# Operand parts made at each head's end and passed through DRAM, states in x tiles, embedding copies first

## The chip, the cores and the metric

The kernel runs on one core of a Trainium2 chip. The metric is the device time of one execution in microseconds (us). The core has TensorE (PE, matmuls, with its weight loads shown apart as PEld), VectorE (DVE), ScalarE (ACT), GpSimd (POOL) and SyncE (SP), each with an instruction queue of its own that is worked off in order. A DMA is issued from one of these queues; a DMA instruction that has to wait for something holds up everything behind it in the same queue.

## The reference, cut to what matters

One step of a two-layer decoder on 512 prompt tokens and 8 x 8 sample tokens (576 columns in all). Per layer:

```python
h = rmsnorm(x, pre_g) @ w_in                 # pool inputs and gates, q, k, v, head gates
u = (causal window mean(h_pool) - h_pool) @ w_pool[g] * pool_scale * silu(gate)   # 4 pool groups
q, k = rope(q), rope(k) * DK ** -0.5         # 4 retention heads of width 256
o = masked(q k^T) v + (q S) * q_decay        # S: (8, 4, 256, 256) states for the samples
S_new = exp(C * log_g) * S + (k * k_decay)^T v
o = head_rmsnorm(o) * silu(gate)             # what a head puts out
m = rmsnorm(concat(u, o) @ w_out, post_g)
x = x + m
ple = rmsnorm(p @ w_ple, ple_g)              # per-layer embedding, 256 -> 2048
x = x + ple * sigmoid(x @ w_ple_gate + b)
```

The outputs are y, the new states of all heads and the last pool rows.

## The kernel before

Everything is held with features on the 128 partitions and the 576 tokens along the free axis: a tile is 128x576, and the width of 2048 is 16 tiles. Every weight matmul is made in three passes in fp32r: a value is split into a high part (ACT casts it, line 91) and a low part (DVE subtracts, line 92), and high by high, high by low and low by high are added up in PSUM, in column halves of 288 (HN). `gemm` (line 137) does this plainly; `unit` (lines 117 to 119) works on blocks of two tiles and on sums of blocks (`block_sums`, lines 190 to 193), so that fewer products are needed; `plain_unit` is line 233. Weights come as raw loads of 1 MB into two buffers and are split into `wh` and `wl`.

A layer runs in stages; the times are those of layer 0 in the profiled execution:

- `in_first` (0 to 290 us): the first half of the input projection; its results go to DRAM.
- `in_phase`, heads (290 to 590 us): four calls of `head(h)`. Each finishes its part of the projection, turns q and k, makes scores and outputs, and calls `retention_state` for the sample tokens. That works in two rounds (`bg`) of four states each. A round loads four states of 256 KB into tiles of `s0_ring` (four slots, m24 to m27), multiplies them with q (line 385), makes the k-v products (line 401), adds them onto the states in place (line 402) and stores the states (line 403). So the second round's loads into the same four slots wait for the first round's stores to have read them. At its end a head normalises, multiplies its two output tiles o[0], o[1] by their gates (line 681), stores them in `m_dram` (line 682), makes two tiles of block sums in `x` buffers and stores these too (line 686).
- `in_phase`, pool (590 to 735 us): four calls of `pool_group`. After each, `operands` (line 749) loads one head's two output tiles and two sums into `x` buffers and splits them into seven slots (`own_slots`) for the output projection.
- `out_phase`: the output projection by `unit` (735 to 871 us), the embedding (871 to 909 us), first half of the gate (909 to 1003 us, `gate_step`), second half (1003 to 1105 us, `gated`). Layer 1 follows (1105 to 2194 us).

In the embedding each of 16 tiles is a `gemm` of 12 matmuls. From its two PSUM halves ACT squares (line 342) and then copies into a `part` buffer (line 801), and SP stores that (line 802). PE sums the squares over the partitions (line 304). In `gated`, the stored embedding tile is loaded into an `x` buffer, DVE scales it (828), adds the accumulators (834), ACT makes the sigmoid (836), DVE multiplies and adds (837, 838), and SP stores the result.

Buffers by name: x 4, tmp 4, part 4, d 4, u 6, raw 2, wh 5, wl 5; `rot_ring` is m16 to m23; PSUM has acc 4, pb 2, po 2. The order of the instructions on each engine is set before the run by a scheduler with a cost model of its own: code moved in the source, another buffer or another queue can move any of them. Nearly all DMAs are issued on SP's queue, one of them on ACT's and none on POOL's.

Of the kernel before, what the change touches and what calls it, by code (L numbers as in the profile page):

```python
# [14 lines left out]
P = 128  # L15
# [23 lines left out]
def decoder_kernel(ctx: ExitStack, tc: tile.TileContext, a, decay8):  # L39
# [6 lines left out]
    def buf(tag, shape=(P, NT), dt=F32):  # L46
        return sb.tile(list(shape), dt, tag=tag, name=tag, bufs=BUFS.get(tag, 1))
# [32 lines left out]
    def dram(name, n=KT):  # L80
        return [tc.dram_tile([P, NT], F32, name=f"{name}{i}") for i in range(n)]
# [4 lines left out]
    sums_dram = [dram(f"sums{l}", 8) for l in range(L)]  # L86
# [127 lines left out]
    def operands(xs, pairs=range(4), ops=None, tag="u", slots=own_slots, sums=None):  # L214
        ops = operand_set() if ops is None else ops
        for j in pairs:
            blocks(xs, [j], ops, slots)
            sums_of_blocks(ops, [j], tag, sums=sums)
        return ops
# [155 lines left out]
    def retention_state(l, h, s0_ring, qrep, kst, vst, po_s):  # L375
        for bg in range(2):
            s0s, loads = [], []
            for r in range(4):
                s0 = s0_ring.tile((P, 2, DK))
                loads.append(nc.sync.dma_start(out=s0, in_=a["state_ret"][l, 4 * bg + r, h].rearrange("(t p) e -> p t e", p=P)))  # L380
                s0s.append(s0)
# [115 lines left out]
    def in_phase(l, raws, r2, rB, cos, sin):  # L497
# [90 lines left out]
        def head(h):  # L588
# [91 lines left out]
            for i, g in enumerate(silu_gates(20 + h)):  # L680
                nc.vector.tensor_tensor(out=o[i], in0=o[i], in1=g, op=ALU.mult)
                nc.sync.dma_start(out=m_dram[l][8 + 2 * h + i], in_=o[i])
            sums = [buf("x") for _ in range(2)]
            block_sums(nc.vector, *o, *sums)
            for i, t in enumerate(sums):
                nc.sync.dma_start(out=sums_dram[l][2 * h + i], in_=t)
# [54 lines left out]
        for j, g in enumerate(groups):  # L741
            pool_group(g)
            operands(loader(m_dram[l][8:]), [j], out_ops, sums=loader(sums_dram[l]))
        return out_ops

    def loader(tiles):
        def xs(k):
            t = buf("x")
            nc.sync.dma_start(out=t, in_=tiles[k])
            return t  # L750
        return xs

    def out_phase(l, raws, ops_out):
# [38 lines left out]
        for c8 in range(2):  # L792
            raw = load_weights(a["w_ple"][l, :, c8 * 8:(c8 + 1) * 8].rearrange("p c k n -> p (c k) n"))
            w = split_weights(raw, 0, 16)
            for c in range(8):
# [3 lines left out]
                square(sq, acc)  # L799
                for i in range(2):  # L800
                    nc.scalar.copy(half(t, i), acc[i])
                nc.sync.dma_start(out=ple_dram[l][ct], in_=t)
# [22 lines left out]
        def gated(ct, t, acc, by_half):  # L825
            pl = buf("x")
            nc.sync.dma_start(out=pl, in_=ple_dram[l][ct])
            nc.vector.scalar_tensor_tensor(
# [55 lines left out]
        next_ops = operand_set() if l < L - 1 else None  # L884
        for p in range(8):
# [116 lines left out]
```

## Time and profile before

| what | us |
|---|---|
| three executions, median (lowest to highest) | 2201.31 (2197.42 to 2420.12) |
| the profiled execution | 2196.17 |
| its span in the trace | 2194.4 |
| PE busy | 2169.6 |
| DVE busy | 1721.7 |
| ACT busy | 1061.0 |
| POOL busy | 89.7 |

The span is the time from the first to the last instruction of the profiled execution; the remaining 1.8 us lie around it. Busy is the time in which an engine worked on an instruction; the span less PE's busy time is the time in which no matmul ran. The granted TensorE clock was 1.00 of full speed in every stage.

### The profile page before, as it was taken

Reading aid. Unit: us, or ns where it says so; the run is one execution under the profiler, and the core shown is the slowest. Engines: PE = TensorE matmul, PEld = TensorE weight load, DVE = VectorE, ACT = ScalarE, POOL = GpSimd, SP = SyncE. Lnnn points to the kernel's source line nnn. Section 1 sums busy time; section 2 is a strip of 40 time slices with the busy share of each in tenths; the row PEclk is TensorE's granted clock in tenths of the full one; section 3 lists DMA queues with packets and bytes.
Section 4 is the critical chain, followed back from the end, with each engine's and each line's share of the span. In section 5 each row is a group of like instructions: output and inputs, shape, how many; then the busy total and the mean of one; then the engine's idle time right before and its main releaser. Section 6 shows DMA issues by size and latency. Waiting matters only on the chain.

```text
span 2194.4 us, 42681 instructions
## 1 busy us (share of the span) xinstructions
PE 2169.6 (99%) x16716; PEld 2138.4 (97%) x16716; DVE 1721.7 (78%) x3186; ACT 1061.0 (48%) x2097; POOL 89.7 (4%) x66
## 2 busy tenths in 40 slices
PE   9999999999999999999999999999999999999998
PEld 9999999999999999999999999999999999999998
DVE  8788765767599998888877787666675898988865
ACT  5465533444344555755454554433443445556532
POOL 2000000000001110000110000000000001101000
PEclk9999999999999999999999999999999999999999
DMA  7455455555574433656644544555464743336564
GB/s 233 144 195 167 156 170 158 168 171 172 169 241 150 133 123 119 215 172 217 205 159 151 168 159 151 159 173 169 149 202 148 250 154 122 110 117 228 178 202 146
DMA packets 143337, 371.42 MB, mean 169 GB/s; under 512 B 15008, under 2 KB 53408, under 8 KB 122272
## 3 DMA queue, kind: packets, MB, share of 16 engines
q1 hardware_dynamic: 142992, 368.69, 50.9%
q8 instruction: 131, 2.15, 0.4%
q14 instruction: 70, 0.57, 0.1%
q10 hardware_dynamic: 144, 0.02, 0.0%
HBM read 277.89 MB, written 90.76 MB: 168 GB/s over the span
## 4 chain that ended last, share of the span: by engine, by line
PE 86%; DMA 6%; DVE 4%; issue 1%; ACT 1%; SPq 0%; POOL 0%; DVEq 0%; ACTq 0%; POOLq 0%
PE acc L137 29%; PE acc L117 13%; PE acc L118 13%; PE acc L119 13%; PE acc L233 4%; PE pb L118 3%; PE pb L117 3%; PE pb L119 3%; DMA x<-ple 2%; DMA out_new_ret_s<-m 2%; PE po L137 1%; PE po L385 1%; DVE wl L92 1%; DMA m<-in_state_ret 1%; DVE x L837 1%
## 5 line engine op out<-in xcount | busy, mean ns | idle before, releaser
L137 PE MATMUL acc<-m,wh 128*128 128x288 f32 x3584 | 649.7, 297 | 0.0
L91 ACT CAST wh<-raw 128x512 fp32r<-128x512 f32 x567 | 351.0, 620 | 534.7 <-PE acc L137 274.5
L118 PE MATMUL acc<-m,wh 128*128 128x288 f32 x1944 | 572.6, 295 | 0.0
L117 PE MATMUL acc<-m,wh 128*128 128x288 f32 x1944 | 570.9, 295 | 0.5 <-ACT m L256 0.5
L119 PE MATMUL acc<-m,wl 128*128 128x288 f32 x1944 | 566.5, 295 | 0.0
L137 PEld LDWEIGHTS acc<-m,wh 128*128 128x128 f32 x3584 | 531.8, 188 | 7.1 <-issue 6.2
L92 DVE TENSOR_TENSOR wl<-raw,wh 128x512 fp32r<-128x512 f32 x567 | 400.9, 708 | 122.7 <-ACT wh L91 118.7
L137 PE MATMUL acc<-m,wl 128*128 128x288 f32 x1792 | 391.4, 295 | 0.0
L117 PEld LDWEIGHTS acc<-m,wh 128*128 128x128 f32 x1944 | 364.5, 188 | 1.5 <-ACT m L256 1.0
L118 PEld LDWEIGHTS acc<-m,wh 128*128 128x128 f32 x1944 | 365.0, 188 | 0.0
L119 PEld LDWEIGHTS acc<-m,wl 128*128 128x128 f32 x1944 | 362.5, 188 | 0.2 <-DVE wl L92 0.2
L91 ACT CAST wh<-S 128x512 fp32r<-128x512 f32 x356 | 220.9, 620 | 239.0 <-PE acc L118 146.1
L137 PEld LDWEIGHTS acc<-m,wl 128*128 128x128 f32 x1792 | 290.0, 188 | 1.4 <-issue 1.4
L92 DVE TENSOR_TENSOR wl<-S,wh 128x512 fp32r<-128x512 f32 x356 | 253.1, 713 | 22.6 <-ACT wh L91 21.5
L246 POOL TENSOR_TENSOR S<-raw 128x512 f32<-128x512 f32 x45 | 70.7, 1572 | 1912.0 <-DMA raw<-in_w_out 752.7
L512 DVE TENSOR_TENSOR part<-acc,part 128x288 f32<-128x288 f32 x192 | 79.1, 451 | 73.7 <-PE acc L137 73.1
L246 DVE TENSOR_TENSOR S<-raw 128x512 f32<-128x512 f32 x133 | 93.4, 702 | 19.0 <-DMA raw<-in_w_in 17.5
L118 PE MATMUL pb<-m,wh 128*128 128x288 f32 x324 | 95.5, 295 | 0.0
L117 PE MATMUL pb<-m,wh 128*128 128x288 f32 x324 | 95.1, 294 | 0.0
L119 PE MATMUL pb<-m,wl 128*128 128x288 f32 x324 | 95.0, 293 | 0.0
L256 ACT COPY d<-acc 128x288 f32<-128x288 f32 x228 | 86.2, 395 | 0.0
L261 DVE TENSOR_TENSOR d<-d,acc 128x288 f32<-128x288 f32 x114 | 51.3, 450 | 36.0 <-PE acc L119 35.6
(269 smaller groups left out, 3286.1 us busy)
## 6 DMA issues: line engine op xcount, KB each, us to landing
raw<-in_w_in SPq DMA_DIRECT2D x95, 1024.0 KB, 5.4
raw<-in_w_out SPq DMA_DIRECT2D x32, 1024.0 KB, 4.9
raw<-in_w_gate SPq DMA_DIRECT2D x32, 1024.0 KB, 5.5
proj<-d SPq DMA_DIRECT2D x96, 288.0 KB, 2.1
part<-proj SPq DMA_DIRECT2D x96, 288.0 KB, 3.2
m<-in_state_ret SPq DMA_DIRECT2D x64, 256.0 KB, 3.0
out_new_ret_s<-m SPq DMA_DIRECT2D x64, 256.0 KB, 5.1
x<-m SPq DMA_DIRECT2D x48, 288.0 KB, 3.4
```

The source lines that it names most:

```text
L91: nc.scalar.copy(hi, src)
L92: return nc.vector.tensor_tensor(out=lo, in0=src, in1=hi.bitcast(F32), op=ALU.subtract)
L117: nc.tensor.matmul(out, wh, xh, start=start, stop=False, **kw)
L118: nc.tensor.matmul(out, wh, xl, start=False, stop=False, **kw)
L119: nc.tensor.matmul(out, wl, xh, start=False, stop=stop, **kw)
L137: nc.tensor.matmul(acc[h], u, v[:, h * HN:(h + 1) * HN], start=(i == 0 and passno == 0), stop=(i == n - 1 and passno == 2),)
L233: nc.tensor.matmul(acc[h], w[:, j], xs[h][passno == 1], start=(i == 0 and j == 0 and passno == 0), stop=(i == 1 and j == 3 and passno == 2),)
L246: eng.tensor_tensor(out=s, in0=x, in1=y, op=op)
L256: ops["tail_act"] = nc.scalar.copy(dst, src)
L261: return nc.vector.tensor_tensor(out=dst, in0=dst, in1=src, op=ALU.add)
L385: mm = nc.tensor.matmul(po_s[32 * r:32 * r + 32, bg], qrep[:, dt, b * 32:b * 32 + 32], s0s[r][:, dt], start=(dt == 0), stop=(dt == 1),)
L512: nc.vector.tensor_tensor(out=half(t, h), in0=acc[h], in1=half(t, h), op=ALU.add)
```

## The change

- At a head's end the two sums go to `tmp` buffers. The first half of o[0], o[1] and the two sums are split there into high and low parts, in `x` buffers: seven tiles of 128x576 (the first holds both parts of a half). They are stored in DRAM (`operand_dram`), by DMAs on POOL's queue. o[0] and o[1] themselves and the sums are no longer stored.
- After each pool group `load_operands` loads the seven tiles of one head into the seven slots, again on POOL's queue, and nothing is split there.
- The second round of four states goes into `x` buffers and not into `s0_ring`.
- In the embedding ACT copies first, POOL's queue stores the copy, and the square is made from the copy in SBUF, as one operation of 576 columns.
- In the second half of the gate the embedding tiles are loaded by code that stands two tiles ahead.

```diff
--- before.py
+++ after.py
@@ -83,7 +83,7 @@
     x_dram, m_dram = dram("x"), [dram(f"m{l}") for l in range(L)]
     ple_dram = [dram(f"ple{l}") for l in range(L)]
     gate_dram = [dram(f"gate{l}") for l in range(L)]
-    sums_dram = [dram(f"sums{l}", 8) for l in range(L)]
+    operand_dram = [[tc.dram_tile([P, NT], F32R, name=f"operand{l}_{i}") for i in range(28)] for l in range(L)]
     proj_dram = [dram(f"proj{l}", 48) for l in range(L)]
 
     def split(hi, lo, src, scale=None):
@@ -211,11 +211,11 @@
                 ops[n2].append((hi[:, HN:], lo[:, HN:]))
         return ops
 
-    def operands(xs, pairs=range(4), ops=None, tag="u", slots=own_slots, sums=None):
+    def operands(xs, pairs=range(4), ops=None, tag="u", slots=own_slots):
         ops = operand_set() if ops is None else ops
         for j in pairs:
             blocks(xs, [j], ops, slots)
-            sums_of_blocks(ops, [j], tag, sums=sums)
+            sums_of_blocks(ops, [j], tag)
         return ops
 
     def plain_unit(raw, ops, d0, d1):
@@ -376,7 +376,7 @@
         for bg in range(2):
             s0s, loads = [], []
             for r in range(4):
-                s0 = s0_ring.tile((P, 2, DK))
+                s0 = buf("x", (P, 2, DK)) if bg else s0_ring.tile((P, 2, DK))
                 loads.append(nc.sync.dma_start(out=s0, in_=a["state_ret"][l, 4 * bg + r, h].rearrange("(t p) e -> p t e", p=P)))
                 s0s.append(s0)
             for dt in range(2):
@@ -679,11 +679,29 @@
 
             for i, g in enumerate(silu_gates(20 + h)):
                 nc.vector.tensor_tensor(out=o[i], in0=o[i], in1=g, op=ALU.mult)
-                nc.sync.dma_start(out=m_dram[l][8 + 2 * h + i], in_=o[i])
-            sums = [buf("x") for _ in range(2)]
+            sums = [tmp() for _ in range(2)]
             block_sums(nc.vector, *o, *sums)
-            for i, t in enumerate(sums):
-                nc.sync.dma_start(out=sums_dram[l][2 * h + i], in_=t)
+            both = buf("x", (P, 2, HN), F32R)
+            split(both[:, 0], both[:, 1], o[0][:, :HN])
+            nc.gpsimd.dma_start(out=operand_dram[l][7 * h], in_=both.rearrange("p a n -> p (a n)"))
+            for i, src in enumerate([o[1]] + sums):
+                parts = [buf("x", (P, NT), F32R) for _ in range(2)]
+                split(*parts, src)
+                for k, part in enumerate(parts):
+                    nc.gpsimd.dma_start(out=operand_dram[l][7 * h + 1 + 2 * i + k], in_=part)
+
+        def load_operands(j, ops):
+            new = own_slots(j)
+            tiles = []
+            for i in range(7):
+                t = new[i]((P, NT))
+                nc.gpsimd.dma_start(out=t, in_=operand_dram[l][7 * j + i])
+                tiles.append(t)
+            ops["b11"].append((tiles[0][:, :HN], tiles[0][:, HN:]))
+            for i, names in enumerate((("b21", "b22"), ("t1", "t2"), ("t3", "t4"))):
+                hi, lo = tiles[1 + 2 * i:3 + 2 * i]
+                for h, name in enumerate(names):
+                    ops[name].append((half(hi, h), half(lo, h)))
 
         def pool_group(g):
             w = WINDOWS[g]
@@ -740,7 +758,7 @@
         out_ops = operand_set()
         for j, g in enumerate(groups):
             pool_group(g)
-            operands(loader(m_dram[l][8:]), [j], out_ops, sums=loader(sums_dram[l]))
+            load_operands(j, out_ops)
         return out_ops
 
     def loader(tiles):
@@ -796,10 +814,10 @@
                 ct = c8 * 8 + c
                 acc = gemm(w[2 * c:2 * c + 2], pp)
                 t, sq = buf("part"), buf(("tmp", "tmp", "tmp", "tmp", "g", "g", "u", "u")[ct % 8])
-                square(sq, acc)
                 for i in range(2):
                     nc.scalar.copy(half(t, i), acc[i])
-                nc.sync.dma_start(out=ple_dram[l][ct], in_=t)
+                nc.gpsimd.dma_start(out=ple_dram[l][ct], in_=t)
+                last_square[0] = nc.scalar.activation(sq, t, AF.Square)
                 squares.append(sq)
                 if len(squares) == 4:
                     together(sums, squares, ct == 3, ct == KT - 1)
@@ -822,9 +840,15 @@
             stats["ss"] = buf("long")
         rP = buf("long")
 
-        def gated(ct, t, acc, by_half):
+        def load_embedding(ct):
             pl = buf("x")
             nc.sync.dma_start(out=pl, in_=ple_dram[l][ct])
+            return pl
+
+        def gated(ct, t, acc, by_half):
+            if ct + 2 < KT:
+                pls.append(load_embedding(ct + 2))
+            pl = pls[ct]
             nc.vector.scalar_tensor_tensor(
                 out=pl, in0=pl, scalar=vec["ple_g"][:, l, ct:ct + 1], in1=rP, op0=ALU.mult, op1=ALU.mult
             )
@@ -882,6 +906,7 @@
             return mo[k]
 
         next_ops = operand_set() if l < L - 1 else None
+        pls = [load_embedding(ct) for ct in range(2)]
         for p in range(8):
             raw = raws.pop(("gate2", p))
             for c in range(2):
```

On the whole SP has 96 DMAs fewer and POOL 144 more. Where the order moves:

PE in head 0 of layer 0 before: the first round of states (m_4423 to m_4429) in its last rows; then the projection goes on, and the second round stands 64 rows further down.

```order
L385 MATMUL po<-m_4427,u 32x256
L385 MATMUL po<-m_4429,u 32x256
L401 MATMUL pb<-u 128x256 x2
L137 MATMUL acc<-m_1850,wh 128x288 x2
L137 MATMUL acc<-m_1851,wh 128x288 x2
L137 MATMUL acc<-m_1850,wl 128x288 x2
```

PE at the same place after:

```order
L385 MATMUL po<-m_4467,u 32x256
L385 MATMUL po<-m_4469,u 32x256
L401 MATMUL pb<-u 128x256 x2
L385 MATMUL po<-x,u 32x256 x8
L137 MATMUL acc<-m_1890,wh 128x288 x2
L137 MATMUL acc<-m_1891,wh 128x288 x2
```

The eight matmuls on the second round's states now stand directly behind those on the first round's. In heads 1 to 3 no row stands between the two.

SP's queue in head 3 before (the buffer numbers show which tile is meant):

```order
L403 DMA out_new_ret_s<-m27_7108 128x2x256
L403 DMA out_new_ret_s<-m24_7110 128x2x256
L380 DMA m27_7150<-in_state_ret 128x2x256
L380 DMA m24_7152<-in_state_ret 128x2x256
L103 DMA raw_7700<-in_w_in2 128x2048
L403 DMA out_new_ret_s<-m25_7112 128x2x256
L403 DMA out_new_ret_s<-m26_7114 128x2x256
L380 DMA m25_7154<-in_state_ret 128x2x256
L380 DMA m26_7156<-in_state_ret 128x2x256
```

and after:

```order
L380 DMA x_7244<-in_state_ret 128x2x256
L506 DMA part_7719<-proj014_259 128x576
L380 DMA x_7246<-in_state_ret 128x2x256
L380 DMA x_7248<-in_state_ret 128x2x256
L103 DMA raw_7645<-in_w_in2 128x2048
L506 DMA part_7802<-proj015_260 128x576
L380 DMA x_7250<-in_state_ret 128x2x256
L403 DMA out_new_ret_s<-m27_7202 128x2x256
```

The second round's loads stood behind the first round's stores; now they stand ahead of them, among the loads of the projection. The four `x` buffers that they fill held the last four parts of head 2.

DVE at the end of head 2 before, from the second sum on, with head 3's first two score tiles (line 629):

```order
L528 TENSOR_TENSOR g_7350<-part_7288,long_2890 128x576
L192 TENSOR_TENSOR x_6530<-m23_6199,m22_6198 128x288
L191 TENSOR_TENSOR x_6529<-m23_6199,x_6529 128x288
L92 TENSOR_TENSOR wl_7530<-raw_6922,wh_7529 128x512
L629 TENSOR_TENSOR tmp_7024<-pb_7017,mask_6537 128x512
L193 TENSOR_TENSOR x_6530<-m23_6199,x_6529 128x288
L92 TENSOR_TENSOR m13_7027<-tmp_7024,m12_7026 128x512
L629 TENSOR_TENSOR tmp_7043<-pb_7036,mask_6537 128x384
```

and after:

```order
L193 TENSOR_TENSOR tmp_6604<-m23_6275,tmp_6603 128x288
L512 TENSOR_TENSOR part_7382<-acc_7392,part_7382 128x288
L512 TENSOR_TENSOR part_7382<-acc_7393,part_7382 128x288
L92 TENSOR_TENSOR wl_7638<-raw_7016,wh_7637 128x512
L92 TENSOR_TENSOR x_6620<-tmp_6603,x_6619 128x576
L528 TENSOR_TENSOR g_7444<-part_7382,long_2930 128x576
L92 TENSOR_TENSOR x_6626<-tmp_6604,x_6625 128x576
L92 TENSOR_TENSOR wl_7642<-raw_7016,wh_7641 128x512
L629 TENSOR_TENSOR tmp_7118<-pb_7111,mask_6631 128x512
```

All splits of head 2's results now stand ahead of head 3's first score tile. Seven parts take turns in four `x` buffers: x_6609, the first, and x_6613 and x_6614 give theirs to x_6620, x_6625 and x_6626.

POOL's queue there, after (before, it has nothing there):

```order
L691 DMA operand0_15_204<-x_6613 128x576
L686 DMA operand0_14_203<-x_6609 128x576
L691 DMA operand0_17_206<-x_6619 128x576
L691 DMA operand0_16_205<-x_6614 128x576
L691 DMA operand0_19_208<-x_6625 128x576
L691 DMA operand0_18_207<-x_6620 128x576
L698 DMA m20_7897<-operand0_5_194 128x576
L698 DMA m21_7899<-operand0_6_195 128x576
L691 DMA operand0_20_209<-x_6626 128x576
```

The seventh store stands behind two loads, into slots m20 and m21 of `rot_ring`.

ACT at the start of layer 0's embedding before:

```order
L342 ACTIVATE tmp<-acc 128x288 x2
L801 COPY part<-acc 128x288 x2
L342 ACTIVATE tmp<-acc 128x288 x2
L801 COPY part<-acc 128x288 x2
L342 ACTIVATE tmp<-acc 128x288
L801 COPY part<-acc 128x288
```

and after:

```order
L818 COPY part<-acc 128x288
L91 CAST wh<-raw 128x512
L344 ACTIVATE tmp<-m_9977 128x576
L344 ACTIVATE tmp<-m_9978 128x576
L818 COPY part<-acc 128x288 x3
L91 CAST wh<-raw 128x512
L818 COPY part<-acc 128x288
L820 ACTIVATE tmp<-part 128x576 x3
```

A tile's two copies (line 818 of the changed kernel) now stand ahead, and the first three squares (line 820) follow four tiles' copies.

In the second half of layer 1's gate DVE, SP and PE have the same rows in the same order before and after: the loads of the embedding tiles stand where they stood.

## Rows read from the trace of the kernel before

**Rows 1.** The page: length of the span, and busy time of each engine.

```profile
span 2194.4 us, 42681 instructions
PE 2169.6 (99%) x16716; PEld 2138.4 (97%) x16716; DVE 1721.7 (78%) x3186; ACT 1061.0 (48%) x2097; POOL 89.7 (4%) x66
```

**Rows 2.** Stages: PE, PEld, DVE, ACT, POOL busy; PE clock, DMA share, GB/s.

```profile
290.00:590.00 300.00, 295.26 (x2315) 286.13 (x2314) 196.57 (x398) 117.20 (x239) 0.00 (x0) 1.00 0.52 164
590.00:735.00 145.00, 144.74 (x1105) 144.13 (x1104) 130.34 (x269) 68.86 (x136) 9.89 (x6) 1.00 0.57 191
735.00:871.00 136.00, 136.00 (x1031) 135.62 (x1030) 127.41 (x223) 71.25 (x127) 13.38 (x10) 1.00 0.34 113
871.00:909.00 38.00, 35.37 (x361) 32.52 (x359) 26.19 (x50) 31.64 (x90) 1.06 (x1) 1.00 0.74 265
...
1960.00:1997.00 37.00, 34.94 (x354) 32.71 (x347) 26.95 (x50) 30.62 (x88) 0.59 (x1) 1.00 0.73 261
```

**Rows 3.** What PE waited for, whole span: us in total, times, longest.

```profile
PE po L385 <- DMA m<-in_state_ret: 6.6, 5, 3.0
PE acc L137 <- ACT part L801: 2.3, 3, 1.0
PE po L304 <- ACT tmp L342: 2.2, 2, 1.1
PE acc L137 <- DVE part L834: 1.7, 1, 1.7
PE po L385 <- issue: 1.2, 2, 0.7
...
PE po L137 <- ACT u L91: 0.9, 1, 0.9
```

**Rows 4.** Chain of waits in head 3 of layer 0: start us, us, what.

```profile
574.24 9.36 DMA out_new_ret_s<-m
...
583.66 3.33 DMA m<-in_state_ret
...
587.24 1.07 PE po L385 x16
```

**Rows 5.** DMA issues: count, KB each, median us from issue to landing.

```profile
m<-in_state_ret SPq DMA_DIRECT2D x64, 256.0 KB, 3.0
...
ple<-part SPq DMA_DIRECT2D x32, 288.0 KB, 3.8
...
sums<-x SPq DMA_DIRECT2D x16, 288.0 KB, 4.7
```

**Rows 6.** DVE by time, head 3 of layer 0: start us, us of work.

```profile
551.04 0.68 DVE L629 TENSOR_TENSOR tmp<-pb,mask 128x512 f32<-128x512 f32 x1
```

**Rows 7.** PE by time, same head, first round of states.

```profile
567.63 1.07 PE L385 MATMUL po<-m,u 128*32 128x256 f32 x16
```

**Rows 8.** Groups by line and shape: busy us, mean ns of one, idle before.

```profile
L801 ACT COPY part<-acc 128x288 f32<-128x288 f32 x64 | 25.6, 430 | 1.7 <-DMA ple<-part 1.5
...
L92 DVE TENSOR_TENSOR m<-x,m 128x576 fp32r<-128x576 f32 x32 | 23.9, 752 | 5.5 <-ACT m L91 5.5
...
L91 ACT CAST m<-x 128x576 fp32r<-128x576 f32 x32 | 21.3, 673 | 22.9 <-DMA x<-sums 14.7 <-DMA x<-m 6.6 <-DVE x L191 0.8
```

**Rows 9.** ACT by time in the embedding of layer 0: start, us of work.

```profile
870.32 1.26 ACT L344 ACTIVATE tmp<-m 128x576 f32<-128x576 f32 x2
871.49 0.60 ACT L91 CAST wh<-raw 128x512 fp32r<-128x512 f32 x1
...
884.33 0.41 ACT L801 COPY part<-acc 128x288 f32<-128x288 f32 x1
884.64 0.41 ACT L342 ACTIVATE u<-acc 128x288 f32<-128x288 f32 x1
```

**Rows 10.** Chain of waits in the last stage, second half of layer 1's gate.

```profile
2165.55 0.34 SPq L840
...
2165.94 3.92 DMA x<-ple
```

## The prediction

> **What bounds the kernel now.** I read the page first. PE is busy for 2169.6 of 2194.4 us [rows 1], so all time in which no matmul runs is 24.8 us, 1.1% of the span. The stage table says what a busy PE means here: in the output projection 1031 matmuls fill 136.00 of 136.00 us, 132 ns each [rows 2]. The change removes no matmul (the order has as many before and after), and the granted clock is 1.00 in all stages. So nothing that only takes waits away can give more than 24.8 us, and faster by 2%, which is about what a measurement of this kernel tells from no change (44 us), is out of reach. The other engines have room on average, DVE 78% and ACT 48% [rows 1], and in the heads less is asked of them: DVE 196.57 of 300.00 us, ACT 117.20, POOL nothing [rows 2].
>
> Then the table of PE's waits. The largest is line 385, the matmuls on the loaded states: 6.6 us in five waits for the load and 1.2 us in two that no release explains [rows 3]. The chain shows how it comes about in head 3: the store of updated states takes 9.36 us until it has landed, only then the load of the second round starts into the freed slot, 3.33 us, and PE's matmuls follow at 587.24 [rows 4]. The embedding comes next: 2.3 us on line 801 (the copies that free the accumulators) and 2.2 us on line 304, which waits for the squares [rows 3]. That is nearly all the idle time of PE in the two embedding stages, 38.00 - 35.37 + 37.00 - 34.94 = 4.7 us [rows 2]. The end of the last stage has one wait of 1.7 us, the pool stage one of 0.9 us [rows 3].
>
> **The change part by part**, against the profiled execution of 2196.2 us.
>
> *States in x buffers.* The second round's loads no longer wait for the first round's stores. That takes away the 6.6 us and with them the 1.2 us that stand at the same matmuls: -7.8 us, with -6.6 as the smaller end. What is late next are the `x` buffers themselves: they come free when POOL's stores of the head before have read them. In head 3 the last split stands just ahead of the first score tile, which DVE takes at 551.04 [rows 6]; the matmuls, now directly behind those on the first round, stand at 567.63 [rows 7]. So there are 16.6 us for the last store and a state load. A load takes 3.0 us, and a store of such a tile from `x` buffers takes 4.7 us when SP issues it [rows 5], together 7.7; with the 9.36 us that a state's store once took [rows 4] it is 12.7 with the load's 3.33. Both fit. The last store also stands behind two loads on POOL that need slots read by head 3's PE; those reads come 144 rows of PE, about 144 x 0.132 = 19 us, ahead of the state matmuls, so that fits as well. SP's queue waits at these loads, with a load of 1 MB of weights behind them; by the same count the weights are late only if the stores are.
>
> *Parts made at the head's end.* Three splits of 576 columns and half a one of 288 move there: DVE 3.5 x 0.752 = 2.6 us, ACT 3.5 x 0.673 = 2.4 us per head [rows 8]. The same work is gone from the pool stage. DVE has some 26 us per head without work and ACT 46 (a quarter of 300.00 less 196.57 and 117.20), so as a sum it is hidden. As a place it is not: DVE's splits stand ahead of the next head's first score tile, and the fifth to seventh wait for the first three stores, because seven parts share four buffers. Behind that wait on DVE are a weight part and the score tile, and PE waits for both. From the first split to the fifth there are nine other operations, some 6 us at 0.68 each [rows 6]; a store takes 4.7 us from SP [rows 5], and POOL issues the first one second. So a wait of 0 to 2 us is near. The six ends with a next head behind them could cost from nothing to 3 us each (all of the 2.6 us uncovered), 0 to 18 us. PE's filler, projection matmuls between the score tiles, hides most of it before; I take 0.5 us each, **+3 us**, near the lower end, since the store row and the room agree to within a microsecond.
>
> *Loads in place of splits after a pool group.* Per layer DVE and ACT lose 10.5 and 9.4 us in a stage where DVE was busy for 130.34 of 145.00 [rows 2]. PE there was idle for 0.3 us only in layer 0, so there is nothing to win but the one wait of 0.9 [rows 3], for the pool weights' split: their load now stands ahead on a shorter SP queue. **-0.9 us**, between -0.9 and 0. The loads wait on POOL; behind them stand its block sums for the output projection, of which the stage has only 9.89 us [rows 2].
>
> *Embedding.* On ACT nothing is saved: two squares and two copies of 288 columns start 0.31 us apart [rows 9], 1.24 us per tile; now two copies and one square of 576 columns (0.58 us, half of 871.49 - 870.32 [rows 9]) make 1.20. But the two accumulators come free after two operations, not after four. The 2.3 us on line 801 go; the 2.2 us on line 304 may stay, as the squares come later: **-2.3 us**, between -4.7 (all) and +2.2 (line 304 doubles). The store's place is a rival below.
>
> *Second half of the gate.* The order of layer 1's last stage is the same row for row: each load of an embedding tile still stands behind the store of an earlier result, as the chain shows (SP at 2165.55 and the load at 2165.94 [rows 10]), because four `x` buffers allow no more. **0 us**; the 1.7 us stay.
>
> *Traffic.* Each head stores seven tiles and loads seven in place of four and four: 48 tiles of 288 KB more in all, 14 MB. The DMA engines are busy for 0.52 to 0.57 of these stages [rows 2], so it is hidden: 0.
>
> Sum: -7.8 + 3.0 - 0.9 - 2.3 = -8.0, so 2196.2 - 8.0 = 2188.2. The median of three was 2201.3, 5 us above the profiled execution, and the lowest 2197.4; I predict **2188 us**, 0.6% below the median.
>
> **The rivals.**
>
> *The x buffers take it back* (2196): stores from POOL land a few microseconds later than SP's, each of the six ends costs 1.8 us and not 0.5, and the 7.8 us are given back. For it: 6 us of room against 4.7. Against: PE has some 140 rows to do between the head's end and its matmuls on states.
>
> *All of PE's waits in these stages go* (2181): -7.8 - 4.7 - 0.9 with the heads' ends hidden make -13.4, and with the 1.7 us of the gate, if less traffic ahead of it should move them, -15.1: 2181. Against: a square now needs its copy first, and the gate's order is as before.
>
> *Slower: POOL's transfers follow each other too slowly* (2218 at 3.0 us each). No DMA of the trace goes through POOL. If it passes one on every p us, the embedding, 2.3 us per tile (37 or 38 us by 16 [rows 2]), is paced by it from p = 2.3 on, once the four `part` buffers are full. The heads have seven stores to make in the 16.6 us of room and the 6 us of the splits, less the load's 3.0, which is 19.6: they are late from p = 2.8 on. At 3.0 the embedding pays 0.7 x 32 = 22 us and the six heads 6 x (21.0 - 19.6) = 8: 2188 + 30 = 2218. At 2.6 it is 10 us, 2198; over 2% slower it is from p = 3.35 on. For it: the copies already waited 1.5 us for SP's stores [rows 8], which land in 3.8 us [rows 5]. Against: a POOL operation over 512 columns took 13.38 / 10 = 1.34 us in the output projection [rows 2], and to issue a transfer need not be more.
>
> *DVE holds POOL's issues up* (2250). If POOL could prepare a transfer only while DVE is idle, the embedding's 38.00 - 26.19 = 11.8 us without DVE work [rows 2] would stretch POOL's 1.34 us to 1.34 x 38 / 11.8 = 4.3 us per store, 16 x 4.3 = 69 us against 38, 31 us more in each layer: 2188 + 62 = 2250. Against: in the output projection POOL made ten operations of 1.34 us while DVE was busy for 127.41 of 136.00 us [rows 2], where it would have had no room for them. The Trainium skill, page "SBUF — State Buffer", under "The 'DVE blocks DMA' trap (SWDGE)", says that the descriptors of a DMA issued from GpSimd can't be written while DVE runs an operation in a two-port mode, and advises SP or ACT as issuers. By that rule this rival comes about if DVE's splits and sums run in that mode; the row of the output projection speaks against it, though a plain POOL operation is no descriptor write, and no run so far shows one.
>
> *It does not do what it says.* For the gate's early loads that is built in: they don't move. If they did, the 1.7 us would go, 2186; it has no chance of its own.
>
> **How the numbers follow.** The forecast (2184 to 2193) 0.48; the x buffers take it back (to 2200) 0.20; all waits gone 0.10; POOL too slow 0.14, some two thirds of it below p = 3.35 and a third below 2.8; DVE in the way 0.03; anything else 0.05. The range from 2177 to 2208 holds the first three and the mild end of the fourth (p up to 2.85), some 0.82. Faster by over 2% (below 2157) lies beneath PE's busy time: 0.01. Slower by over 2% (above 2245) is the hard end of POOL's rival, DVE's, and the unforeseen: 0.05 + 0.03 less what of these stays under it, and something of the rest, 0.07. Within 2%: 0.92.
>
> **What would show it.** PE's waits for the state loads should be gone from the table, and the copies' wait in the embedding too; the wait at the last stage's end should still be there. The group that decides is DVE's splits at the heads' ends: idle time ahead of line 92 on `x`, released by POOL's stores, is the first rival. In the DMA table the POOL-issued stores should land in 4 to 6 us; 8 us or more means the third. PE's busy time should stay within 1 us. I would be wrong if the new order makes PE wait where the trace of before shows no wait at all: at the score tiles, at the squares, or for weights behind SP's loads into `x`.

## The result and the profile after

The changed kernel takes 2185.36 us as the median of six executions (2184.24 to 2191.19), where the kernel before, beside it, takes 2199.35. One of its six executions there took 2420.12 us, a slow one, which the ratio leaves out. The ratio is 0.995 with a 95% interval of 0.9937 to 0.9962: 8 to 14 us faster, 0.5%, which lies within the 2% that the chances speak of and clear of the measurement's own spread. 2188 was predicted.

The page of the profiled execution (2186.74 us), as in [rows 1]:

```profile
span 2184.8 us, 42838 instructions
PE 2168.9 (99%) x16716; PEld 2138.1 (98%) x16716; DVE 1726.2 (79%) x3186; ACT 1063.6 (49%) x2065; POOL 178.5 (8%) x210
```

PE works as long as before (2168.9 for 2169.6 us). Its time without work fell from 24.8 to 15.9 us, and that is 8.9 of the 9.6 us by which the span is shorter. What PE waits for now, beside [rows 3]:

```profile
PE acc L137 <- DVE part L858: 2.3, 2, 1.2
PE acc L233 <- DVE part L858: 1.8, 3, 0.9
PE acc L233 <- DVE m L92: 1.3, 3, 0.6
...
PE acc L119 <- DVE wl L92: 0.7, 2, 0.3
...
```

Lines 385, 801 and 304 are gone from the table, and so is the wait in the pool stage: 6.6 + 1.2 + 2.3 + 2.2 + 0.9 = 13.2 us. In exchange 4.3 us came back, most of them in the gate. Line 834, now 858, has 4.1 us for 2.3; the gate's first operand (line 233 for the split of line 92) has 1.3 where there was none; smaller ones, 0.7 of them on a weight part (line 119), bring the rest. The stages, with the columns of [rows 2]:

```profile
290.00:590.00 300.00, 300.00 (x2365) 290.60 (x2364) 209.13 (x427) 130.00 (x260) 18.89 (x35) 1.00 0.60 191
590.00:735.00 145.00, 144.74 (x1096) 144.50 (x1095) 124.50 (x249) 61.74 (x121) 22.36 (x27) 1.00 0.56 180
...
871.00:909.00 38.00, 37.11 (x368) 35.25 (x367) 29.59 (x60) 27.67 (x64) 7.77 (x13) 1.00 0.67 228
...
1378.00:1675.00 297.00, 297.00 (x2342) 287.60 (x2341) 208.07 (x428) 129.78 (x260) 18.77 (x35) 1.00 0.60 189
```

The heads have no gap at all on PE any more, in either layer, although DVE and ACT each have some 13 us more to do there. POOL's transfers, by issue and landing, are as follows (count, KB each, median us to landing); the last line is the second round's state loads:

```profile
operand<-x POOLq DMA_DIRECT2D x56, 288.0 KB, 3.3
m<-operand POOLq DMA_DIRECT2D x56, 288.0 KB, 5.5
...
ple<-part POOLq DMA_DIRECT2D x32, 288.0 KB, 4.7
...
x<-in_state_ret SPq DMA_DIRECT2D x32, 256.0 KB, 4.2
```

And the timeline of POOL at the end of head 2 (start us, us, what, idle time before and its releaser), with the instructions that waited for the operand tiles below it:

```profile
541.66 0.54 POOL L691 DMA_DIRECT2D operand<-x  x1 [64.91 <-ACT x L91]
542.25 0.53 POOL L686 DMA_DIRECT2D operand<-x  x1
543.14 1.12 POOL L691 DMA_DIRECT2D operand<-x  x2 [0.37 <-ACT x L91]
546.18 1.12 POOL L691 DMA_DIRECT2D operand<-x  x2 [1.91 <-ACT x L91]
...
548.78 0.54 POOL L691 DMA_DIRECT2D operand<-x  x1
```

```profile
  ACT x L91: 8.0, 4
  DVE x L92: 0.7, 1
```

A store takes POOL 0.54 us, and the seven are spread over some 7 us because six of them wait for the splits and the seventh stands behind two loads. The splits did wait for buffers, 8.7 us in all, but PE waited for none of them.

### The profile page after: what moved, and what is told of

Read it like the earlier page. It is cut to its first block, busy times and chain, and to the rows that moved or that the text cites. A ratio compares the mean times of both kernels' runs of the same rounds, so it can differ in the third digit from the quotient of the medians.

```text
span 2184.8 us, 42838 instructions
## 1 busy us (share of the span) xinstructions
PE 2168.9 (99%) x16716; PEld 2138.1 (98%) x16716; DVE 1726.2 (79%) x3186; ACT 1063.6 (49%) x2065; POOL 178.5 (8%) x210
## 4 chain that ended last, share of the span: by engine, by line
PE 90%; DVE 4%; DMA 3%; issue 1%; ACT 1%; SPq 0%; DVEq 0%; ACTq 0%
PE acc L137 34%; PE acc L119 13%; PE acc L118 13%; PE acc L117 13%; PE acc L233 3%; PE pb L118 3%; PE pb L119 3%; PE pb L117 3%; DMA x<-ple 2%; PE po L137 1%; DVE wl L92 1%; PE pb L401 1%; PE po L385 1%; PE pb L577 1%; PE po L327 1%
## 5 line engine op out<-in xcount | busy, mean ns | idle before, releaser
L246 POOL TENSOR_TENSOR S<-raw 128x512 f32<-128x512 f32 x45 | 77.9, 1732 | 650.9 <-DMA raw<-in_w_out 214.6
L691 POOL DMA_DIRECT2D operand<-x x48 | 25.8, 538 | 972.1 <-ACT x L91 965.7
```

The costliest lines, as they stand in the source:

```text
L246: eng.tensor_tensor(out=s, in0=x, in1=y, op=op)
L691: nc.gpsimd.dma_start(out=operand_dram[l][7 * h + 1 + 2 * i + k], in_=part)
```

## The experiments

Each was timed beside the kernel before; a ratio is to that one, with its 95% interval. Three groups of four ran on different occasions, and the median of before was 2195.6, 2197.7 and 2197.8 us in them. The changed kernel was timed once, for the result above, with the ratio 0.995 (0.9937 to 0.9962); where a run is compared with it, its microseconds come from another occasion, and the ratios are the safer measure. The diffs are cut to the lines that matter.

**States alone.** The kernel before, with:

```diff
-                s0 = s0_ring.tile((P, 2, DK))
+                s0 = buf("x", (P, 2, DK)) if bg else s0_ring.tile((P, 2, DK))
```

> The kernel before with one edit: the second round of four states is loaded into x buffers. Theory (the parts of the change add up, each with its own place): PE's 7.8 us at line 385 go and nothing else moves by more than 1 us, so 6 to 9 us faster than before, about 2191.5. Rival (the x buffers are only free in time because the operand parts left the SP queue): the loads into x wait for the stores and loads of the sums, line 385 keeps 4 us or more of its wait, and the gain is under 4 us.

2190.12 us, ratio 0.9971 (0.9959 to 0.9983), 4 to 9 us faster. Line 385 is gone from PE's waits, and no other of its lines grew by more than 0.3 us. PE's busy time grew by 2.9 us in this trace, some 1.8 of them from one fall of the granted clock behind a wait of 1.7 us (shown in the last section). The theory holds for the wait and the time: this wait ends with the buffers alone, even while the sums still go through `x`. That the parts add up, as it also says, the next runs refute.

**Operand parts alone.** The kernel before, with the heads' ends and the loads after the pool groups as in the change:

```diff
-            operands(loader(m_dram[l][8:]), [j], out_ops, sums=loader(sums_dram[l]))
+            load_operands(j, out_ops)
```

> The kernel before with the operand parts alone: splits at the heads' ends, stores and loads on POOL's queue; states, embedding and gate as before. Theory: PE's waits at line 385 stay at 6 to 8 us, the heads' ends cost PE nothing, the wait of 0.9 us in the pool stage goes; time between 2 us faster and 1 us slower than before. First rival (what was predicted, the heads' ends cost about 0.5 us each): PE waits at the score tiles or for weights in the heads, 3 us or more in the sum, 2 to 3 us slower. Second rival (the shorter SP queue is what helps): line 385 loses half of its wait or more, 4 us faster or better.

2210.37 us, ratio 1.0054 (1.0033 to 1.0075): slower, by more than any of the three expected. The six executions fall into two near 2201.5 and four near 2210. PE's longest waits in the traced one (2201.7 us):

```profile
PE acc L137 <- DVE part L512: 6.2, 4, 2.9
...
PE po L385 <- issue: 0.8, 2, 0.5
PE po L385 <- DMA m<-in_state_ret: 0.7, 2, 0.4
```

The heads' ends cost PE 0.9 us (a score tile's split), not 3. Line 385 keeps only 1.5 of its 7.8 us, so the state loads do come earlier without the sums on SP's queue, as the second rival had it, though its 4 us did not come. That the queue's length is what helps them was not traced. But the pool stage has something new: PE waits for line 512, DVE's addition that frees the accumulators, up to 2.9 us at a time. In the chain of waits DVE starts that stretch late, for a load of the projection (3.25 us from 634.86), which itself starts only when DVE's line 528 is done with its buffer; behind its line 512 DVE then has nine microseconds of the pool group's work in its queue ahead of the next one:

```profile
634.86 3.25 DMA part<-proj
...
647.69 0.38 DVE part L512
```

**Embedding alone.** The kernel before, with the embedding's edit:

```diff
-                square(sq, acc)
                 for i in range(2):
                     nc.scalar.copy(half(t, i), acc[i])
-                nc.sync.dma_start(out=ple_dram[l][ct], in_=t)
+                nc.gpsimd.dma_start(out=ple_dram[l][ct], in_=t)
+                last_square[0] = nc.scalar.activation(sq, t, AF.Square)
```

> The kernel before with the embedding's edit alone: copies first, square from the copy in SBUF, store on POOL's queue. Theory: of PE's 4.7 us without work in the two embedding stages under 1.5 are left, 3 to 4.7 us faster there; the new waits behind it in the first half of the gate (1 to 3 us in the changed kernel) come from this part and show here, so 1 to 4 us faster in all. Rival (those waits come from the other parts): line 233 waits as long as before, under 2 us, and the whole 3 to 4.7 us show.

2194.85 us, ratio 0.9992 (0.9979 to 1.0004): no change in time that can be told, where the theory had 1 to 4 us. In the two embedding stages it holds: PE's idle time there is 1.4 us for 4.7. Lines 801 and 304 are gone from the waits, 4.5 us. New are:

```profile
PE acc L233 <- DVE m L92: 1.4, 3, 0.6
...
PE pb L119 <- DVE wl L92: 0.6, 1, 0.6
```

The wait of line 233 for line 92 thus comes with this part; line 834, at 1.9 us, has not grown here. The chain of the changed kernel shows what is late next there: the residual's loads.

```profile
888.62 5.55 DMA x<-in_x
...
894.87 0.37 DVE m L92
...
895.54 0.75 DVE m L92
...
897.62 0.67 PE acc L233 x3
```

**The same with the stores on SP.** Its edit undoes the queue:

```diff
-                nc.gpsimd.dma_start(out=ple_dram[l][ct], in_=t)
+                nc.sync.dma_start(out=ple_dram[l][ct], in_=t)
```

> As the run before it, but the embedding's stores stay on SP's queue. Theory (the order of copy and square frees the accumulators, the queue does not matter): PE's idle time in the two embedding stages within 1 us of the run with POOL's queue, time within 1.5 us of it. Rival (POOL's queue did it, since SP's held the stores up behind loads): idle time in these stages stays at 3 us or more, and 2 us or more slower than the run with POOL's queue.

2197.57 us, ratio 1.0004 (0.9991 to 1.0017). The waits on 801 and 304 are gone here too, so the order of copy and square did that, as in the theory. But PE's idle time in the two embedding stages is 38.00 - 35.37 + 37.00 - 35.51 = 4.1 us, where the run with POOL's queue has 1.4: not within 1 us, as the theory had it, but over the rival's 3.

```profile
871.00:909.00 38.00, 35.37 (x349) 32.73 (x351) 26.40 (x49) 31.09 (x72) 0.00 (x0) 1.00 0.75 239
1960.00:1997.00 37.00, 35.51 (x364) 33.02 (x363) 26.91 (x51) 30.98 (x71) 0.00 (x0) 1.00 0.75 249
```

Most of it is a new wait, at the gate's first products:

```profile
PE acc L233 <- ACT part L800: 2.9, 2, 2.0
```

In layer 0 the chain of waits shows how it comes about. On SP a load of the residual stands behind a store of the embedding that waits for ACT's copies; it starts at 896.01 and takes 6.44 us. DVE waits for it, ACT waits 2.4 us for DVE, and the copies that PE needs stand behind that on ACT. So on SP's queue the store does hold up a load here. The two medians are 2.7 us apart with intervals that overlap, so the time does not settle it; a later run, with the states and the parts in the kernel too, shows that the queue is worth less than 2 us there.

**States and operand parts together**, embedding and gate as before the change (the two edits above in one kernel).

> The kernel before with the states in x buffers and the operand parts together; embedding and gate as before. The parts alone gave 0.54% slower, the states alone 0.29% faster; their sum would be 0.25% slower than before, about 2201 where before is 2196. Theory (the two parts work on each other: with the parts alone the order of SP's queue in the pool stage puts a load of the projection behind a store and PE waits there for 6 us, and with both the order has no such place): PE's waits on line 512 in the pool stage are gone, line 385's too, 6 to 10 us faster than before. Rival (they add up, and the changed kernel's gain comes from embedding and gate): slower than before by 2 us or more, with the waits on line 512 still there.

2185.79 us, ratio 0.9952 (0.9938 to 0.9965): 8 to 14 us faster, the whole gain of the change, so that the embedding and the gate add nothing to it that can be told. The waits on line 512 and 385 are gone; what is left (in the traced execution, at 2191.58 us the longest of the six):

```profile
PE acc L137 <- DVE part L852: 3.1, 3, 1.5
PE po L304 <- ACT tmp L342: 2.2, 2, 1.1
PE acc L137 <- ACT part L819: 1.9, 2, 1.0
PE pb L119 <- DVE wl L92: 1.2, 1, 1.2
```

So the parts do not add up: one alone 0.54% slower, the other 0.29% faster, both 0.48% faster. That the operand parts bring anything beyond the states is not shown, since the intervals of the last two overlap; what is clear is that they no longer cost their 12 us. With both, DVE has other rows around the pool groups, and the late stretch does not come about. Why the scheduler puts them so was not traced.

**Twice the stores.** The changed kernel with every store of a part made twice, into the same DRAM tile:

```diff
-                    nc.gpsimd.dma_start(out=operand_dram[l][7 * h + 1 + 2 * i + k], in_=part)
+                    for _ in range(2):
+                        nc.gpsimd.dma_start(out=operand_dram[l][7 * h + 1 + 2 * i + k], in_=part)
```

> The changed kernel with each of the seven stores at a head's end made twice into the same DRAM tile (twice the load on POOL's queue; what is computed is unchanged). Theory (the heads' ends have room: PE has other matmuls in between, and POOL takes about half a microsecond per store): splits wait longer for their buffers, 15 us or more in the sum over ACT and DVE where it was 9, but PE waits less than 2 us more in the heads; within 3 us of the changed kernel. Rival (there is just enough room, as the prediction had it): PE waits at the score tiles or for the states, 1 to 3 us at each of six ends, 6 us or more slower than the changed kernel.

2187.43 us, ratio 0.9952 (0.9938 to 0.9966), the same as the changed kernel. The splits' waits grew from 8.7 to 17.6 us:

```profile
  DVE x L92: 10.9, 6
  ACT x L91: 6.7, 2
```

and the state loads now came late, at the last head of each layer:

```profile
PE po L385 <- DMA x<-in_state_ret: 2.8, 2, 1.7
```

This lies between the two: PE waits, 0.8 us more than the theory allowed, yet in two places and not in six, and the time does not show it. The room at the heads' ends is thus about as large as seven further stores need (1.1 us of the wait are in layer 0 and 1.7 in layer 1).

**Eight buffers in the gate.** The changed kernel with:

```diff
-            pl = buf("x")
+            pl = buf("tmp" if l == L - 1 and ct % 2 else "x")
```

> The changed kernel, where in layer 1 every second embedding tile of the gate's second half is loaded into a tmp buffer, so that eight buffers take turns and not four. Theory (the early loads of the changed kernel move nothing because four x buffers allow no more): the loads stand ahead of the stores, PE's two waits of 2.3 us at the end go, and DVE is not late after the last matmul: 2 to 4 us faster than the changed kernel. Rival (DVE's own order, which scales a tile three tiles ahead of its use, keeps the end as it is): DVE still waits 40 us or more for embedding tiles, no change within 1 us.

2186.55 us, ratio 0.9956 (0.9944 to 0.9969): nothing gained, as the rival had it for the time. Its reason is not the one: DVE's waits for embedding tiles fell from 47.1 us in the changed kernel to 35.4, and the waits at the end of layer 1 did go, as the theory had it. Two in the first half of layer 1's gate took their place, one of 0.8 us and this one:

```profile
PE acc L119 <- DVE wl L92: 2.6, 1, 2.6
```

**All transfers on SP.** The changed kernel with POOL's 144 transfers issued on SP (the parts seen as plain float32 by the transfer, same bytes):

```diff
-                    nc.gpsimd.dma_start(out=operand_dram[l][7 * h + 1 + 2 * i + k], in_=part)
+                    nc.sync.dma_start(out=operand_dram[l][7 * h + 1 + 2 * i + k], in_=part.bitcast(F32))
```

> The changed kernel with all of POOL's DMAs issued on SP instead (144 DMAs go back to SP's queue). Theory (POOL's queue matters, because a store that waits for a split holds up what stands behind it on SP, the loads of weights and of the projection): PE waits more in the heads or the pool stage, 3 to 15 us slower than the changed kernel. Rival (the queue does not matter, since the scheduler puts the DMAs in the order in which they can go): within 2 us of the changed kernel.

2183.84 us, ratio 0.9944 (0.9928 to 0.9961). The rival holds: the queue does not matter, within 2 us. The splits waited 0.8 us for their buffers and not 8.7, and the stores land sooner from SP (2.7 us for 3.3), but PE had not waited for the splits before either. The heads have no gap here:

```profile
290.00:590.00 300.00, 300.00 (x2365) 290.60 (x2364) 208.98 (x427) 130.00 (x260) 0.00 (x0) 1.00 0.59 191
```

**Without the early loads** in the gate (that part of the changed kernel put back):

```diff
-            if ct + 2 < KT:
-                pls.append(load_embedding(ct + 2))
-            pl = pls[ct]
+            pl = buf("x")
+            nc.sync.dma_start(out=pl, in_=ple_dram[l][ct])
```

> The changed kernel without its early loads of the embedding tiles in the gate (that part as before the change). Theory (they move nothing that matters): within 1.5 us of the changed kernel, PE's waits on the gate's line 834 within 1 us of the 4.1 us that line 858 has in the changed kernel, the others of the gate as there. Rival (they brought the new waits of layer 0's gate): these waits fall to the 2.3 us of the kernel before, 2 us faster than the changed kernel.

2184.47 us, ratio 0.9936 (0.992 to 0.9952): by its median 0.9 us below the changed kernel, by the ratios 3 us, with intervals that overlap. The gate's waits on its additions are 3.2 us for 4.1. The early loads gave nothing; whether they cost 1 to 3 us is below what was measured.

**The gate's second buffers filled by POOL.** The changed kernel with:

```diff
-            pl = buf("x")
-            nc.sync.dma_start(out=pl, in_=ple_dram[l][ct])
+            other = l == L - 1 and ct % 2
+            pl = buf("tmp" if other else "x")
+            (nc.gpsimd if other else nc.sync).dma_start(out=pl, in_=ple_dram[l][ct])
```

> The changed kernel, where in layer 1 every second embedding tile of the gate is loaded into a tmp buffer by POOL's queue, so that SP's queue keeps its order. Theory (with eight buffers on SP's queue the loads stood ahead of weights and cost there what they gave at the end): no wait of PE over 1 us in layer 1's gate, neither for a weight part in its first half nor at the end; 2 to 4 us faster than the changed kernel. Rival (PE's end does not hang on it): within 1 us of the changed kernel.

2190.42 us, ratio 0.9964 (0.9951 to 0.9976): slower than the changed kernel, if anything. The wait in the first half of layer 1's gate is still there, 3.3 us, so SP's order was not its only cause. The chain names what held it up here:

```profile
2009.22 4.00 DMA tmp<-ple
...
2013.24 0.04 DVE tmp L853
...
2013.98 0.75 DVE m L92
...
2016.65 0.70 DVE wl L92
...
2017.39 0.61 PE acc L119
```

With early tiles the scheduler also puts DVE's scaling of them (line 853) earlier, into the first half of the gate. DVE stands there for a load of 4.00 us, and the splits and weight parts for PE stand behind it. My theory fell.

**The last two edits together**, with all other transfers on SP.

> All of the changed kernel's POOL transfers on SP, and in layer 1 every second embedding tile of the gate loaded into a tmp buffer by POOL's queue: the two best of the earlier runs together. Expected if they add up: 0 to 2 us from the first and 2 to 4 us from the second, 0.7% faster than the kernel before; if the first was chance, as the run with the gate's edit alone.

2188.01 us, ratio 0.9954 (0.9941 to 0.9967): they don't add up, and the wait for the weight part in layer 1's gate is there again (3.5 us). No version tried is clearly faster than the changed kernel.

**Operand parts alone, again.**

> The operand parts alone once more, for a second trace: four of its six executions took about 2210 us and two 2201.5, the traced one 2201.7. Theory (the long waits of PE in the pool stage differ from execution to execution, and a fall of the granted clock behind them makes them dearer): in an execution near 2210 the waits on line 512 are longer or more, and the clock falls more than twice. Rival (something else than PE's waits): the same waits as in the first trace and the time lies in longer matmuls elsewhere. If the trace is again one near 2201, it tells nothing.

2209.24 us, ratio 1.0049 (1.0035 to 1.0063); the traced execution took 2209.8. Its waits and three stretches of 20 us (columns as in [rows 2]):

```profile
PE acc L137 <- DVE part L512: 8.0, 4, 2.9
PE acc L137 <- DVE part L852: 4.0, 3, 2.1
```

```profile
640.00:660.00 20.00, 17.11 (x119) 16.91 (x119) 15.72 (x38) 5.84 (x12) 0.00 (x0) 0.91 0.42 138
1720.00:1740.00 20.00, 17.40 (x120) 17.18 (x119) 11.67 (x27) 4.84 (x10) 2.53 (x5) 0.91 0.87 285
2180.00:2200.00 20.00, 17.93 (x122) 17.50 (x121) 11.37 (x19) 3.73 (x6) 0.00 (x0) 0.91 0.29 90
```

The theory holds. The waits are longer than in the first trace, a long one at the end of the last stage (line 852) has come to them, and the granted clock has a mean of 0.91 in the stretch of each long wait, three times where the first trace had it in two of these. A mean of 0.91 over 20 us is some 3.6 us at 1.2 GHz in place of 2.4, and about 1.8 us of work given up. The two traces' 8.2 us of difference are 4.4 of idle time on PE and 3.8 of longer matmuls; the third fall would explain some 1.8 of these, and the other 2 were not traced.

## Why the prediction was right, point by point

- **The bound.** PE's idle time and no more can go: so it was, 8.9 us of idle time and 0.7 of busy time. Over 2% was out of reach.
- **States**, -7.8: exactly these 7.8 us left the table of waits. Alone the edit gave 4 to 9 us. The room for the last store and load, 16.6 us by the rows, was there; it closed only with twice the stores, at the last heads.
- **Heads' ends**, +3: measured 0. This term was mis-sized. What it rests on did come, the splits waited 8.7 us for their buffers, but PE's other matmuls covered all of it (300.00 of 300.00 us busy). The first rival, that this would eat the gain, thus fell.
- **Pool loads**, -0.9: the wait is gone. With the states alone it is already down to 0.3 us, so it is not shown that the loads did it.
- **Embedding**, -2.3: both waits went, 4.5 us. Line 801 went as forecast. Line 304 went because the scheduler put PE's first sum of squares later, behind some 120 matmuls of the embedding in place of some 60, by which time the squares were made. But what came next I had not priced: the residual's loads are late behind it, 1.3 us on line 233 (1.4 with this part alone). The 4.3 us that came back in all places have other sources too; line 852, the same addition, has 3.1 us with the states and parts and no edit of the embedding. Alone, this part gave nothing that could be measured. My -2.3 was near the net by two errors that lie in opposite directions, which is luck.
- **Gate**, 0: right. The waits at the end of layer 1 stayed, 2.3 us for 1.7, and without the early loads the time is the same as far as was measured.
- **Traffic**, 0: nothing contradicts it. DMA's share rose from 0.52 to 0.60 in the heads, where PE had no gap.
- **POOL too slow**, and **DVE holds POOL up**: neither came. POOL spends 0.54 us on a transfer, where I had put up to 1.34 and the trouble began at 2.3. Stores from POOL landed in 3.3 and 4.7 us. In the embedding DVE was busy for 29.59 of 38.00 us, and POOL issued its stores beside it; the Trainium skill's rule of the page "SBUF — State Buffer" (section "The 'DVE blocks DMA' trap (SWDGE)") did not bite with DVE's work as it is here, and putting the transfers on SP, as it advises, changed nothing beyond 2 us. Whether any of DVE's operations here runs in the two-port mode that the rule speaks of, no trace shows.

In sum -8.0 was forecast against the profiled execution, and -9.4 is what the two profiled executions differ by (2196.17 and 2186.74). By PE's idle time the sum went otherwise than forecast: -13.2 where I had -7.8 - 0.9 - 2.3 = -11.0, nothing for the heads' ends where I had +3.0, and 4.3 that came back and were in no term. That these nearly cancel is luck. The step that the account lacked altogether is that the parts act on each other through the order of the queues. Added up, the single runs (-6.4, +11.9, -1.8 us) would have made the kernel slower; the two larger ones together gave -10.5. I costed each part against the trace of before as if the order elsewhere stayed. What stands out between 12 us slower and 10 us faster are the waits in the pool stage, which no term named, and the falls of the clock behind them. The second trace of the parts alone is 13.7 us longer than that of before: 5.3 of idle time (8.0 on line 512, while line 385 lost 5.7), and 8.4 of longer matmuls, of which three falls at some 1.8 us each explain 5.4. The rest is not explained.

What stays open: why the scheduler's order in the pool stage is worse with the parts alone; why waits of the same place differ from execution to execution by a microsecond or two; which parts brought the waits that came back in the gate; and what the single parts are worth below some 2 us.

## What to carry to other kernels

Where an engine is 99% busy, add up its waits before any edit: that sum is the ceiling for an edit that only takes waits away, and each wait has one place from which it is released. A new buffer or queue is judged by the order that results in the whole kernel, not by its own place: time the parts together as well as alone, since here one of them was 0.5% slower alone and part of a 0.5% gain together. Under such a scheduler a load made earlier can also move its consumer up in an in-order queue; if the consumer gets there first, it holds up everything behind it.

## What the runs showed of the hardware

A long wait of PE can cost more than itself. In the run with the embedding's stores on SP, PE waited up to 2.4 and 2.1 us for the states in the stretches below, and the granted clock of each has a mean of 0.91. In steps of 1 us the first reads 0.50, the lower of the two levels, from 371 to 373 us, directly behind the wait, and 1.00 from 374 on.

```profile
360.00:380.00 20.00, 17.62 (x132) 16.20 (x131) 11.83 (x22) 4.63 (x8) 0.00 (x0) 0.91 0.73 235
580.00:600.00 20.00, 17.93 (x134) 16.51 (x133) 8.90 (x21) 4.87 (x10) 0.00 (x0) 0.91 0.62 207
```

In the kernel before, the same stretches have idle time of 1.1 and 3.0 us and a clock of 1.00; in the run with the embedding alone, 2.1 and 2.4 us, and 1.00 too:

```profile
360.00:380.00 20.00, 18.86 (x153) 18.13 (x152) 12.82 (x25) 5.85 (x11) 0.00 (x0) 1.00 0.77 251
580.00:600.00 20.00, 16.96 (x150) 16.00 (x148) 10.03 (x23) 6.55 (x13) 0.00 (x0) 1.00 0.62 205
```

With the states alone a wait of 1.7 us in the last stage was enough:

```profile
2140.00:2160.00 20.00, 18.29 (x126) 17.93 (x125) 10.78 (x20) 5.42 (x9) 0.00 (x0) 0.91 0.57 181
```

So a wait of 1.7 to 3 us of PE is followed by a fall of the clock in some traces and not in others. It may be a part of why executions of the kernel before lie between 2190 and 2202 us, but no trace of its slower ones was taken.

With early tiles in the gate, a wait of 3.3 us left a longer stretch at the lower level:

```profile
2010.00:2030.00 20.00, 16.26 (x101) 15.68 (x100) 15.32 (x25) 7.59 (x16) 1.43 (x3) 0.83 0.51 170
```

A transfer issued on POOL takes 0.54 us of its queue. The same transfers on SP take 0.32 us (stores) and 0.38 (loads), and they land sooner: the operand stores in 2.7 us for 3.3, the operand loads in 4.8 for 5.5, the embedding's stores in 4.2 for 4.7. In the time of the kernel none of this could be told.
